# Attention mixer of a two-layer decoder trunk: the norm's scale moved from the qkv weights to the transposed input, the query's norm factor moved into the softmax's scale, the head norms' scales folded into key and cosines

## The chip, the cores and the metric

The kernel runs on one core of a Trainium2 chip. The metric is the device time of one execution in microseconds (us), the median of several runs; lower is better.

## The reference, cut to what matters

Two layers over an input of 256 x 1024 (fp32). Each is: half a gated feed-forward net, a mixer, half a feed-forward net. Layer 0's mixer is a state-space layer, layer 1's is attention with 8 heads of 128. The change touches the attention mixer alone:

```
hn = rms_norm(h, mix_norm[1])                 # h / rms(h) * g, g of 1024
qkv = (hn @ w_qkv).reshape(256, 3, 8, 128)
q = rms_norm(qkv[0], q_gain)                  # over each head's 128, gain of 128
k = rms_norm(qkv[1], k_gain)
q = rope(q, cos, sin) * 128 ** -0.5           # rotates features 0..31, passes 32..127
k = rope(k, cos, sin)
p = softmax(causal(q @ k.T)); o = p @ v;  out = o @ w_out
```

With 256 positions and blocks of 256 there is one block, so the block selection of the reference adds nothing.

## The kernel before, in words

All large products run in three terms. An fp32 operand is split into a high part, rounded to the fast fp32r format, and a low part, the rest; the product is high x high + high x low + low x high. Weights arrive by DMA on the SP queue in units of 1 MB (a tile `raw`, three buffers); `Stream.split` (lines 74 to 98) turns each half unit of 128 x 1024 into `whi` (ScalarE) and `wlo` (VectorE: raw minus whi). A unit that has a gain (the scale of the norm ahead of the product) is scaled on the way, in two pieces of 512 columns, each with its own column of the gain (lines 89 to 94); one without is done in one piece (lines 83 to 87). Splits are issued in program order, by `pump()` at set places and by `get()` where a product needs one that is not there yet.

The residual `h` is transposed by `prep` (line 330): four transposes on TensorE into one PSUM tile, then the high part by ScalarE (342) and the low part by VectorE (343). The factor 1/rms(h) is computed aside (`squares`, `rsq` on GpSimd) and applied when the product leaves PSUM.

`moba` (line 1256) is the attention mixer. It runs twelve chunks in the order k0, q0, k1, q1, v0, v1, each for two row tiles t; a chunk is 128 rows by 512 columns (four heads) and has eight steps k of three products (439 to 441). A chunk with t = 0 meets new weights, one with t = 1 uses the same again. After a chunk ScalarE takes it out of PSUM (`qs`, 1278) and squares each head (1282), and GpSimd makes the head norm's factor `rs` (1283, `rsq` 310 to 314). During the next chunk, ahead of its step 5, `rope` on VectorE multiplies the four heads by factor and gain (1293) and rotates 32 features (1299 to 1304); one chunk later TensorE transposes the result (1314). Scores, their maxima (1324 to 1328), the exponential (1335, 1337), and the product with v are spread over later chunks in slots. Every engine does its work in the order in which the program issues it; nothing is reordered at run time.

Of the kernel before, what the change touches and what calls it, by code (L numbers as in the profile page):

```python
# [10 lines left out]
F32 = mybir.dt.float32  # L11
F32R = mybir.dt.float32r
AF = mybir.ActivationFunctionType
OP = mybir.AluOpType
# [7 lines left out]
EPS = 1e-6  # L22
RAW = 3
HB = 9
NEG = -3.0e38
TWO_PI = 2.0 * math.pi
MAGIC = 12582912.0

# [92 lines left out]
def trunk_kernel(ctx: ExitStack, tc, x, ffn_norm, ffn_w_gate, ffn_w_up, ffn_w_down, mix_norm,  # L121
# [3 lines left out]
    nc = tc.nc  # L125
# [10 lines left out]
    def psM():  # L136
        return pp.tile([128, 512], F32, name="pM", tag="M", bufs=2)

    def psR():
        return pp.tile([128, 512], F32, name="pR", tag="R", bufs=2)  # L140
# [14 lines left out]
    units = []  # L155
    where = {}
    WHOLE = 2
    GAIN = {"f00": None, "f01": 8, "f10": 16, "f11": 24, "s5": 32, "moba": 40}

    def add(key, load, gains=None, whole=False):  # L160

        where[key] = len(units)
        units.append((key, load, gains, whole))
# [27 lines left out]
    def ld_cols(w, r0, c0):  # L191
        def f(t):
            nc.sync.dma_start(t.rearrange("p (k c) -> p k c", c=512),
                              w[r0:r0 + 512, c0:c0 + 512].rearrange("(k p) c -> p k c", p=128))
        return f

    def ffn_units(tag, l, i):
        for j in range(NJ + 1):
            if j < NJ:
                for a in range(2):  # L200
                    add((tag, "g", j, a), ld_gu(l, i, j, a, 2 if j == 0 else 4),
                        GAIN[tag] and GAIN[tag] + 4 * a)
            if j:
                add((tag, "d", j - 1), ld_rows(ffn_w_down[l, i], (j - 1) * 256))

    def s5_units():
        for nh in range(2):
            for a in range(2):
                add(("win", nh, a), ld_cols(s5_w_in[0], a * 512, nh * 512), GAIN["s5"] + 4 * a)
        for key in (('glu', 0), ('glu', 1), ('glu', 2), ('glu', 3), ('so', 0), ('so', 1), ('so', 2), ('so', 3)):  # L210
# [4 lines left out]
    QOFF = {"q": 0, "k": 1024, "v": 2048}  # L215

    def moba_units():
        for kind, hh in QKV:
            for a in range(2):
                add((kind, hh, a), ld_cols(moba_w_qkv[0], a * 512, QOFF[kind] + hh * 512), GAIN["moba"] + 4 * a)  # L220
        for b in range(4):
            add(("mo", b), ld_rows(moba_w_out[0], b * 256))

# [20 lines left out]
    cosT = cst[:, 256:288].rearrange("p (t f) -> p t f", t=2)  # L244
    sinT = cst[:, 288:320].rearrange("p (t f) -> p t f", t=2)
# [45 lines left out]
    gT = cp.tile([128, 48], F32, name="gT")  # L291
# [15 lines left out]
    def rsq(o, v, n):  # L307

        e = sp.tile([128, n], F32, name="rs_e", tag=f"rs_e{n}", bufs=2)
        nc.gpsimd.tensor_tensor(o, v, nhalf[:, 0:n], op=OP.pow)  # L310
        nc.gpsimd.tensor_tensor(e, o, o, op=OP.mult)
        nc.gpsimd.tensor_tensor(e, e, v, op=OP.mult)
        nc.gpsimd.tensor_scalar(e, e, -0.5, 1.5, op0=OP.mult, op1=OP.add)
        nc.gpsimd.tensor_tensor(o, o, e, op=OP.mult)
# [15 lines left out]
    def prep(t, n, ph, sq=True):  # L330

        if (ph, "x") not in X:
            X.clear()
            X[ph, "x"] = True
            X["h"], X["l"] = home(XP[0], ph)
        hh = h[t][:, n * 512:(n + 1) * 512]
        ps = psR()
        pv = ps.rearrange("p (k c) -> p k c", c=128)
        for k in range(4):
            nc.tensor.transpose(pv[:, k, :], hh[:, k * 128:(k + 1) * 128], ident)  # L340
        xh, xl = (X[p][:, n * 4:n * 4 + 4, t * 128:t * 128 + 128] for p in "hl")
        nc.scalar.activation(xh, pv, AF.Copy)
        nc.vector.tensor_tensor(xl, pv, xh.bitcast(F32), op=OP.subtract)
        if sq:
            squares(t, n)

# [909 lines left out]
    def moba(nxt):  # L1256
        V, P = nc.vector, nc.gpsimd
        SCL = 128 ** -0.5
        with tc.tile_pool(name="moba", bufs=1) as wp:
            gq = wp.tile([128, 2, 128], F32, name="gq")  # L1260
            for i, g in enumerate((moba_q_norm, moba_k_norm)):
                nc.sync.dma_start(gq[:, i, :], bass.AP(tensor=g.tensor, offset=g.offset,
                                                       ap=[[0, 128], [1, 128]]))
            vs = [wp.tile([128, D], F32, name=f"vs{t}") for t in range(2)]
            oa = wp.tile([128, 4224], F32R, name="oa")
            oh, ol = (oa[:, OO + 2048 * i:OO + 2048 * i + 2048].rearrange("p (k c) -> p k c", c=256)
                      for i in range(2))
            qkT, QS, QN, SC, PR, PT = {}, {}, {}, {}, {}, {}

            def chunk(kind, hh, t, hooks):  # L1270
                uA, uB = where[kind, hh, 0], where[kind, hh, 1]
                ps = psM()
                product(ps, t, uA, uB, hooks)
                if kind == "v":
                    nc.scalar.activation(halves(vs[t][:, hh * 512:(hh + 1) * 512]), unwoven(ps), AF.Identity, scale=Rr[t])
                    return
                qs = fp.tile([128, 512], F32, name="qs", tag="gr", bufs=2)
                nc.scalar.activation(halves(qs), unwoven(ps), AF.Identity, scale=Rr[t])
                ss = wp.tile([128, 4], F32, name="qss", bufs=2)
                sq = wp.tile([128, 128], F32, name="qsq", bufs=1)  # L1280
                for i in range(4):
                    nc.scalar.activation(sq, qs[:, i * 128:(i + 1) * 128], AF.Square, accum_out=ss[:, i:i + 1])
                P.tensor_scalar(ss, ss, 1.0 / 128, EPS, op0=OP.mult, op1=OP.add)
                rs = wp.tile([128, 4], F32, name="qrs", bufs=2)
                rsq(rs, ss, 4)
                QS[kind, hh, t] = (qs, rs)

            def rope(kind, hh, t):
                qs, rs = QS.pop((kind, hh, t))
                qn = wp.tile([128, 4, 128], F32, name="qn", bufs=2)  # L1290
                g = gq[:, 0 if kind == "q" else 1, :]
                for i in range(4):
                    V.scalar_tensor_tensor(qn[:, i, :], qs[:, i * 128:(i + 1) * 128], rs[:, i:i + 1], g,
                                           op0=OP.mult, op1=OP.mult)
                x1, x2 = qn[:, :, 0:16], qn[:, :, 16:32]
                cb = cosT[:, t, None, :].to_broadcast([128, 4, 16])
                sb = sinT[:, t, None, :].to_broadcast([128, 4, 16])
                m = [wp.tile([128, 4, 16], F32, name=f"rp{i}", bufs=1) for i in range(4)]
                V.tensor_tensor(m[0], x1, cb, op=OP.mult)
                V.tensor_tensor(m[1], x2, sb, op=OP.mult)  # L1300
                V.tensor_tensor(m[2], x2, cb, op=OP.mult)
                V.tensor_tensor(m[3], x1, sb, op=OP.mult)
                V.tensor_tensor(x1, m[0], m[1], op=OP.subtract)
                V.tensor_tensor(x2, m[2], m[3], op=OP.add)
                QN[kind, hh, t] = qn
# [11 lines left out]
            def scores(hd):  # L1317
                hh, i = divmod(hd, 4)
                q, k = qkT["q", hh], qkT["k", hh]
                ps = psA(i)  # L1320
                mm(ps[:, 0:128], q[:, i, 0:128], k[:, i, 0:128], start=True, stop=True)
                mm(ps[:, 128:384], q[:, i, 128:256], k[:, i, 0:256], start=True, stop=True)
                dv = ps.rearrange("p (a c) -> p a c", c=256)[:, :, 0:128]
                V.tensor_tensor(dv, dv, cmask[:, None, :].to_broadcast([128, 2, 128]), op=OP.add)
                mx = wp.tile([128, 2], F32, name="mx", bufs=3)
                V.reduce_max(mx[:, 0:1], ps[:, 0:128], axis=AX.X)
                V.reduce_max(mx[:, 1:2], ps[:, 128:384], axis=AX.X)
                V.tensor_scalar(mx, mx, -SCL, None, op0=OP.mult)
                SC[hd] = (ps, mx)

            def expo(hd):
                ps, mx = SC.pop(hd)
                pr = wp.tile([128, 384], F32, name="pr", bufs=4)
                sm = wp.tile([128, 2], F32, name="sm", bufs=4)
                nc.scalar.activation(pr[:, 0:128], ps[:, 0:128], AF.Exp, bias=mx[:, 0:1], scale=SCL,
                                     accum_out=sm[:, 0:1])
                nc.scalar.activation(pr[:, 128:384], ps[:, 128:384], AF.Exp, bias=mx[:, 1:2], scale=SCL,
                                     accum_out=sm[:, 1:2])
                PR[hd] = (pr, sm)

# [32 lines left out]
            for hd in range(8):  # L1373
                g = 24 + 4 * hd if hd < 4 else 30 + 2 * hd
# [104 lines left out]
    ps = psR()  # L1479
# [31 lines left out]
def host_consts():  # L1511
# [3 lines left out]
    pos = 4 * (r % 32) + r // 32  # L1515
    c[:, 128:256] = np.where(pos[None, :] <= pos[:, None], 0.0, NEG).astype(np.float32)
    inv = (500000.0 ** (-np.arange(0, 32, 2, dtype=np.float64) / 32)).astype(np.float32)
# [34 lines left out]
```

## Time and profile before

| | |
|---|---|
| median of 3 runs | 925.89 us (921.27 to 927.68) |
| the profiled execution | 926.08 us, of which the span is 924.3 |
| TensorE (PE) | 914.9 us, 99% of the span |
| VectorE (DVE) | 719.0 us, 78% |
| ScalarE (ACT) | 587.0 us, 64% |
| GpSimd (POOL) | 222.7 us, 24% |
| TensorE clock granted, mean | 0.997 |

The span runs from the first instruction to the last. Busy shares are means over stages that differ; the attention mixer's projections lie at 642 to 720 us, its output product follows up to about 747.

### The profile page before, as it was taken

What the parts mean: (1) busy time and instruction counts of PE and PEld (TensorE: products, weight loads), DVE (VectorE), ACT (ScalarE), POOL (GpSimd) and SP (SyncE); (2) the same over time, 40 slices, a digit from 0 to 9 for tenths busy, and PEclk for the clock granted to TensorE, in tenths of its full rate; (3) what the DMA queues carried; (4) which work ended last, traced back from release to release, by engine and by line L of the source; (5) the groups of instructions that cost most, each with busy time, mean ns of one, the idle gap of its engine ahead of it and who ended that gap; (6) DMA issues with size and microseconds to landing.
All of it is one profiled execution on the core that took longest, in us unless ns stands there. A gap on an engine that the chain in (4) does not pass through costs nothing.

```text
span 924.3 us, 15612 instructions
## 1 busy us (share of the span) xinstructions
PE 914.9 (99%) x5772; PEld 817.9 (88%) x5772; DVE 719.0 (78%) x1235; ACT 587.0 (64%) x1122; POOL 222.7 (24%) x389
## 2 busy tenths in 40 slices
PE   9999999999999999999999999999999999999998
PEld 7888878898999999999999999999888899999997
DVE  6899877868877888777678887776789668887773
ACT  7665756654376666666466666665898666676651
POOL 6992879924812000000020000001441020000000
PEclk9999999999999999999999999999999999999999
DMA  9999999988746766565637666563554647656531
GB/s 286 277 294 334 331 265 273 301 282 322 287 158 197 235 224 231 186 227 183 183 126 238 228 194 216 186 224 97 182 164 156 195 135 252 234 187 227 182 137 46
DMA packets 145388, 200.75 MB, mean 217 GB/s; under 512 B 20168, under 2 KB 117408, under 8 KB 145056
## 3 DMA queue, kind: packets, MB, share of 16 engines
q1 hardware_dynamic: 137744, 188.24, 62.6%
q0 software_dynamic: 6848, 10.72, 4.3%
q10 hardware_dynamic: 720, 0.80, 0.3%
q8 instruction: 45, 0.74, 0.3%
q14 instruction: 31, 0.25, 0.1%
HBM read 183.82 MB, written 15.76 MB: 216 GB/s over the span
## 4 chain that ended last, share of the span: by engine, by line
PE 89%; DMA 3%; POOL 2%; issue 2%; DVE 2%; ACT 1%; SPq 0%; ACTq 0%; DVEq 0%; POOLq 0%
PE pR L589 11%; PE pM L589 11%; PE pA L425 10%; PE pA L426 10%; PE pA L427 10%; PE pR L591 5%; PE pM L591 5%; PE pM L425 4%; PE pM L426 4%; PE pM L427 4%; PE pM L595 2%; PE pM L596 2%; PE pM L594 2%; DMA dA<-t 2%; PE pR L1118 1%
## 5 line engine op out<-in xcount | busy, mean ns | idle before, releaser
L93 DVE SCALAR_TENSOR_TENSOR wlo<-raw,gT,whi 128x512 fp32r<-128x512 f32 x328 | 228.0, 747 | 41.9 <-ACT whi L92 41.7
L87 DVE TENSOR_TENSOR wlo<-raw,whi 128x1024 fp32r<-128x1024 f32 (+1 forms) x155 | 188.0, 1233 | 41.4 <-ACT whi L86 37.0
L92 ACT ACTIVATE whi<-raw,gT 128x512 fp32r<-128x512 f32 x328 | 212.9, 710 | 3.5 <-PE pA L427 2.1
L86 ACT ACTIVATE whi<-raw 128x1024 fp32r<-128x1024 f32 (+1 forms) x155 | 158.5, 1045 | 38.3 <-DMA raw<-in_ffn_w_up_dram 25.5
L589 PE MATMUL pR<-xa,whi 128*128 128x512 f32 x456 | 174.2, 382 | 0.0
L589 PE MATMUL pM<-xa,whi 128*128 128x512 f32 x456 | 174.0, 382 | 0.0
L425 PE MATMUL pA<-whi,ah 128*128 128x512 f32 x352 | 134.9, 383 | 0.0
L426 PE MATMUL pA<-wlo,ah 128*128 128x512 f32 x352 | 133.7, 380 | 0.0
L427 PE MATMUL pA<-whi,al 128*128 128x512 f32 x352 | 133.6, 379 | 0.0
L591 PE MATMUL pR<-xa,wlo 128*128 128x256 f32 x456 | 124.3, 273 | 0.0
L591 PE MATMUL pM<-xa,wlo 128*128 128x256 f32 x456 | 124.3, 273 | 0.0
L355 POOL TENSOR_TENSOR ms<-ss 128x1 f32<-128x1 f32 x10 | 3.5, 348 | 435.4 <-ACT sq L352 435.4
L589 PEld LDWEIGHTS pR<-xa,whi 128*128 128x128 f32 x456 | 86.2, 189 | 12.2
L589 PEld LDWEIGHTS pM<-xa,whi 128*128 128x128 f32 x456 | 86.2, 189 | 11.9
L591 PEld LDWEIGHTS pM<-xa,wlo 128*128 128x128 f32 x456 | 87.4, 192 | 1.4
L591 PEld LDWEIGHTS pR<-xa,wlo 128*128 128x128 f32 x456 | 87.6, 192 | 0.0
L618 ACT ACTIVATE sg<-gr 128x256 f32<-128x256 f32 x66 | 27.5, 417 | 87.2 <-DVE gr L611 61.6
L425 PE MATMUL pM<-whi,xa 128*128 128x512 f32 (+1 forms) x208 | 79.9, 384 | 0.0
L426 PE MATMUL pM<-wlo,xa 128*128 128x512 f32 (+1 forms) x208 | 76.2, 366 | 0.1
L427 PE MATMUL pM<-whi,xa 128*128 128x512 f32 (+1 forms) x208 | 76.1, 366 | 0.0
L427 PEld LDWEIGHTS pA<-whi,al 128*128 128x128 f32 x352 | 66.7, 189 | 9.5
L425 PEld LDWEIGHTS pA<-whi,ah 128*128 128x128 f32 x352 | 66.8, 190 | 9.3
(290 smaller groups left out, 1745.1 us busy)
## 6 DMA issues: line engine op xcount, KB each, us to landing
raw<-in_ffn_w_down_dram SPq DMA_DIRECT2D x44, 1024.0 KB, 5.5
raw<-in_ffn_w_gate_dram SPq DMA_DIRECT2D x80, 512.0 KB, 4.0
raw<-in_ffn_w_up_dram SPq DMA_DIRECT2D x80, 512.0 KB, 5.1
raw<-in_moba_w_qkv_dram SPq DMA_DIRECT2D x12, 1024.0 KB, 5.2
TB<-dB SPq DMA_DIRECT2D x8, 768.0 KB, 7.0
dA<-blank SPq DMA_DIRECT2D x8, 512.0 KB, 10.2
dB<-tt POOLq DMA_DIRECT2D x16, 256.0 KB, 7.5
raw<-in_s_w_in_dram SPq DMA_DIRECT2D x4, 1024.0 KB, 9.7
```

Source lines behind the costliest of these rows:

```text
L86: nc.scalar.activation(hi[:, c], r[:, c], AF.Copy)
L87: nc.vector.tensor_tensor(lo[:, c], r[:, c], hi[:, c].bitcast(F32), op=OP.subtract)
L92: nc.scalar.activation(hi[:, c], r[:, c], AF.Identity, scale=g)
L93: nc.vector.scalar_tensor_tensor(lo[:, c], r[:, c], g, hi[:, c].bitcast(F32), op0=OP.mult, op1=OP.subtract)
L425: mm(o, xh, wh, start=start, stop=False)
L426: mm(o, xh, wl, start=False, stop=False)
L427: mm(o, xl, wh, start=False, stop=stop)
L589: mm(ps[i], a, XB[:, :, k, :].rearrange("p i (t c) -> p i c t", t=2), start=k == 0, stop=False, skip_group_check=True)
L591: mm(ps[i][:, 0:256], b, xh, start=False, stop=k == 7, skip_group_check=True)
L594: mm(o, a, xh, start=k == 0 and i == 0, stop=False, skip_group_check=True)
L595: mm(o, a, xl, start=False, stop=False, skip_group_check=True)
L618: nc.scalar.activation(sg, gr[:, 0, :], AF.Silu)
```

## The change

The gain of the attention mixer's norm leaves the weight split (its units have none now, and are split in one piece) and goes to `prep`: for this phase each of the four transposed blocks is scaled by its own column of the gain, in four instructions on ScalarE and four on VectorE in place of one each. The query is no longer multiplied by its norm factor and gain: `rope` rotates `qs` in place. The factor, times 128 ** -0.5, goes to a small tile `scl` (one more GpSimd step), which is the scale of the exponential and of the maxima. For the 96 features that are not rotated the query's gain is multiplied into the key's (`gk`); for the 32 rotated ones each gain goes into its own cosines and sines (`cs`). These two tables are made by ten GpSimd instructions at the start of `moba`. The mask's constant is smaller in size, as it is scaled now.

```
-    GAIN = {"f00": None, "f01": 8, "f10": 16, "f11": 24, "s5": 32, "moba": 40}
+    GAIN = {"f00": None, "f01": 8, "f10": 16, "f11": 24, "s5": 32, "moba": None}
...
-                add((kind, hh, a), ld_cols(moba_w_qkv[0], a * 512, QOFF[kind] + hh * 512), GAIN["moba"] + 4 * a)
+                add((kind, hh, a), ld_cols(moba_w_qkv[0], a * 512, QOFF[kind] + hh * 512))
...
-        nc.scalar.activation(xh, pv, AF.Copy)
-        nc.vector.tensor_tensor(xl, pv, xh.bitcast(F32), op=OP.subtract)
+        if ph == "moba":
+            for k in range(4):
+                g = gT[:, 40 + 4 * n + k:41 + 4 * n + k]
+                nc.scalar.activation(xh[:, k, :], pv[:, k, :], AF.Identity, scale=g)
+                nc.vector.scalar_tensor_tensor(xl[:, k, :], pv[:, k, :], g, xh[:, k, :].bitcast(F32),
+                                               op0=OP.mult, op1=OP.subtract)
+        else:
+            nc.scalar.activation(xh, pv, AF.Copy)
+            nc.vector.tensor_tensor(xl, pv, xh.bitcast(F32), op=OP.subtract)
...
+            gk = wp.tile([128, 128], F32, name="gk")
+            P.memset(gk[:, 0:32], 1.0)
+            P.tensor_tensor(gk[:, 32:128], gq[:, 0, 32:128], gq[:, 1, 32:128], op=OP.mult)
+            cs = wp.tile([128, 2, 4, 2, 16], F32, name="cs")
+            for i in range(2):
+                for m, (tr, c) in enumerate(((cosT, 0), (sinT, 16), (cosT, 16), (sinT, 0))):
+                    P.tensor_tensor(cs[:, i, m], tr, gq[:, i, None, c:c + 16].to_broadcast([128, 2, 16]), op=OP.mult)
...
+                if kind == "q":
+                    if t == 0:
+                        SQ[hh] = wp.tile([128, 4, 2], F32, name="scl", bufs=2)
+                    P.tensor_scalar(SQ[hh][:, :, t], rs, SCL, None, op0=OP.mult)
...
-                qn = wp.tile([128, 4, 128], F32, name="qn", bufs=2)
-                g = gq[:, 0 if kind == "q" else 1, :]
-                for i in range(4):
-                    V.scalar_tensor_tensor(qn[:, i, :], qs[:, i * 128:(i + 1) * 128], rs[:, i:i + 1], g,
-                                           op0=OP.mult, op1=OP.mult)
+                qn = qs.rearrange("p (i c) -> p i c", c=128)
+                if kind == "k":
+                    for i in range(4):
+                        V.scalar_tensor_tensor(qn[:, i, :], qn[:, i, :], rs[:, i:i + 1], gk, op0=OP.mult, op1=OP.mult)
...
-                V.tensor_scalar(mx, mx, -SCL, None, op0=OP.mult)
+                V.scalar_tensor_tensor(mx, mx, -1.0, SQ[hh][:, i, :], op0=OP.mult, op1=OP.mult)
...
-                nc.scalar.activation(pr[:, 0:128], ps[:, 0:128], AF.Exp, bias=mx[:, 0:1], scale=SCL,
+                nc.scalar.activation(pr[:, 0:128], ps[:, 0:128], AF.Exp, bias=mx[:, 0:1], scale=sc[:, 0:1],
```

## Rows read from the trace of the kernel before

**Rows 1.** The page, busy time by engine over the whole span.
```profile
PE 914.9 (99%) x5772; PEld 817.9 (88%) x5772; DVE 719.0 (78%) x1235; ACT 587.0 (64%) x1122; POOL 222.7 (24%) x389
```

**Rows 2.** Table by stage: length, busy PE, PEld, DVE, ACT, POOL, clock, DMA, GB/s.
```profile
642.00:700.00 58.00, 57.17 (x287) 48.77 (x286) 46.92 (x136) 52.73 (x139) 26.42 (x60) 1.00 0.49 159
700.00:740.00 40.00, 40.00 (x207) 35.19 (x206) 31.93 (x70) 26.49 (x57) 0.00 (x0) 1.00 0.55 181
```

**Rows 3.** Waits of the weight loads, 640 to 750 us: total, times, longest.
```profile
PEld pM L441 <- DVE wlo L93: 2.4, 4, 0.7
```

**Rows 4.** TensorE in order of time: start, duration, instruction, at the four waits.
```profile
655.70 0.38 PE L439 MATMUL pM<-whi,xa 128*128 128x512 f32 x1
655.91 0.38 PE L440 MATMUL pM<-whi,xa 128*128 128x512 f32 x1
656.54 0.48 PE L441 MATMUL pM<-wlo,xa 128*128 128x512 f32 x1 [0.24 <-DVE wlo L93]
...
667.66 0.38 PE L440 MATMUL pM<-whi,xa 128*128 128x512 f32 x1
668.10 0.48 PE L441 MATMUL pM<-wlo,xa 128*128 128x512 f32 x1
...
681.62 0.38 PE L440 MATMUL pM<-whi,xa 128*128 128x512 f32 x1
682.19 0.48 PE L441 MATMUL pM<-wlo,xa 128*128 128x512 f32 x1 [0.19 <-DVE wlo L93]
...
695.38 0.38 PE L440 MATMUL pM<-whi,xa 128*128 128x512 f32 x1
696.08 0.48 PE L441 MATMUL pM<-wlo,xa 128*128 128x512 f32 x1 [0.33 <-DVE wlo L93]
```

**Rows 5.** Groups by line, 632 to 737 us: busy, mean ns, idle before.
```profile
L93 DVE SCALAR_TENSOR_TENSOR wlo<-raw,gT,whi 128x512 fp32r<-128x512 f32 x47 | 32.7, 746 | 4.1 <-ACT whi L92 4.1
L87 DVE TENSOR_TENSOR wlo<-raw,whi 128x1024 fp32r<-128x1024 f32 x8 | 9.6, 1222 | 5.3 <-ACT whi L86 5.3
...
L92 ACT ACTIVATE whi<-raw,gT 128x512 fp32r<-128x512 f32 x48 | 31.6, 715 | 0.0
L1282 ACT ACTIVATE qsq<-qs 128x128 f32<-128x128 f32 x32 | 9.9, 310 | 1.4
L86 ACT ACTIVATE whi<-raw 128x1024 fp32r<-128x1024 f32 x8 | 8.2, 1047 | 0.0
```

**Rows 6.** VectorE in order of time, 651 to 696 us; xN: merged neighbours.
```profile
651.26 1.42 DVE L93 SCALAR_TENSOR_TENSOR wlo<-raw,gT,whi 128x512 fp32r<-128x512 f32 x2 [2.81 <-ACT whi L92]
653.62 1.14 DVE L1293 SCALAR_TENSOR_TENSOR qn<-qs,qrs,gq 128x128 f32<-128x128 f32 x4 [0.94 <-POOL qrs L314]
...
665.18 1.14 DVE L1293 SCALAR_TENSOR_TENSOR qn<-qs,qrs,gq 128x128 f32<-128x128 f32 x4 [0.93 <-POOL qrs L314]
...
689.99 1.14 DVE L1293 SCALAR_TENSOR_TENSOR qn<-qs,qrs,gq 128x128 f32<-128x128 f32 x4
...
695.28 1.41 DVE L93 SCALAR_TENSOR_TENSOR wlo<-raw,gT,whi 128x512 fp32r<-128x512 f32 x2
```

**Rows 7.** GpSimd in order of time, around the mixer's first chunk.
```profile
646.94 0.19 POOL L314 TENSOR_TENSOR rr<-rr,rs_e 128x1 f32<-128x1 f32 x1
650.70 0.20 POOL L1283 TENSOR_SCALAR qss<-qss 128x4 f32<-128x4 f32 x1 [3.57 <-ACT qsq L1282]
...
652.08 0.65 POOL L311 TENSOR_TENSOR rs_e<-qrs 128x4 f32<-128x4 f32 x1
```

**Rows 8.** GpSimd, line 741: ns min/median/max, first and last start, forms.
```profile
L741 POOL TENSOR_TENSOR e<-sc x4: 238/685/1217, 36.1 to 41.9; 128x32 f32<-128x32 f32 x4
...
L741 POOL TENSOR_TENSOR e<-e,e x2: 251/284/318, 44.0 to 45.4; 128x32 f32<-128x32 f32 x2
```

**Rows 9.** ScalarE's and TensorE's instructions for the fourth half, in time.
```profile
644.37 1.32 ACT L92 ACTIVATE whi<-raw,gT 128x512 fp32r<-128x512 f32 x2
...
647.06 0.38 PE L441 MATMUL pM<-wlo,xa 128*128 128x512 f32 x1
```

More of the change, by code (lines that the diff above doesn't have):

```diff
@@ L24 @@
 HB = 9
-NEG = -3.0e38
+NEG = -1.0e30
 TWO_PI = 2.0 * math.pi
@@ L1267, in moba @@
                       for i in range(2))
-            qkT, QS, QN, SC, PR, PT = {}, {}, {}, {}, {}, {}
+            qkT, QS, QN, SC, PR, PT, SQ = {}, {}, {}, {}, {}, {}, {}
             def chunk(kind, hh, t, hooks):
@@ L1289, in rope @@
                 qs, rs = QS.pop((kind, hh, t))
-                qn = wp.tile([128, 4, 128], F32, name="qn", bufs=2)
-                g = gq[:, 0 if kind == "q" else 1, :]
-                for i in range(4):
-                    V.scalar_tensor_tensor(qn[:, i, :], qs[:, i * 128:(i + 1) * 128], rs[:, i:i + 1], g,
-                                           op0=OP.mult, op1=OP.mult)
+                qn = qs.rearrange("p (i c) -> p i c", c=128)
+                if kind == "k":
+                    for i in range(4):
+                        V.scalar_tensor_tensor(qn[:, i, :], qn[:, i, :], rs[:, i:i + 1], gk, op0=OP.mult, op1=OP.mult)
                 x1, x2 = qn[:, :, 0:16], qn[:, :, 16:32]
-                cb = cosT[:, t, None, :].to_broadcast([128, 4, 16])
-                sb = sinT[:, t, None, :].to_broadcast([128, 4, 16])
+                c1, s2, c2, s1 = (cs[:, "qk".index(kind), k, t, None, :].to_broadcast([128, 4, 16]) for k in range(4))
                 m = [wp.tile([128, 4, 16], F32, name=f"rp{i}", bufs=1) for i in range(4)]
[L1299 to L1302, printed above, removed]
+                V.tensor_tensor(m[0], x1, c1, op=OP.mult)
+                V.tensor_tensor(m[1], x2, s2, op=OP.mult)
+                V.tensor_tensor(m[2], x2, c2, op=OP.mult)
+                V.tensor_tensor(m[3], x1, s1, op=OP.mult)
                 V.tensor_tensor(x1, m[0], m[1], op=OP.subtract)
@@ L1332, in expo @@
                 ps, mx = SC.pop(hd)
+                sc = SQ[hd // 4][:, hd % 4, :]
                 pr = wp.tile([128, 384], F32, name="pr", bufs=4)
                 sm = wp.tile([128, 2], F32, name="sm", bufs=4)
-                nc.scalar.activation(pr[:, 0:128], ps[:, 0:128], AF.Exp, bias=mx[:, 0:1], scale=SCL,
+                nc.scalar.activation(pr[:, 0:128], ps[:, 0:128], AF.Exp, bias=mx[:, 0:1], scale=sc[:, 0:1],
                                      accum_out=sm[:, 0:1])
-                nc.scalar.activation(pr[:, 128:384], ps[:, 128:384], AF.Exp, bias=mx[:, 1:2], scale=SCL,
+                nc.scalar.activation(pr[:, 128:384], ps[:, 128:384], AF.Exp, bias=mx[:, 1:2], scale=sc[:, 1:2],
                                      accum_out=sm[:, 1:2])
```

## The prediction

> **What bounds the kernel now.** I read the page's first part, then a table of the stretch that the change touches, then the waits of TensorE there, then the instructions around each wait. The first part says that TensorE is busy for 99% of the span [rows 1]. An average can hide a stage with another limit, so the second look is at the attention mixer's projections and scores, 642 to 700 us: TensorE 57.17 of 58.00 us, ScalarE 52.73, VectorE 46.92, GpSimd 26.42, clock 1.00 [rows 2]. TensorE bounds this stage too; the other engines are close behind it and are late now and then. How often? The list of waits has one entry that counts: the third product of a step (the one that reads wlo) waited for VectorE's split four times, 2.4 us at the weight loads [rows 3]. The four places are seen as a late start after the second product: 0.63, 0.44, 0.57 and 0.70 us where 0.215 is usual, so 0.41 + 0.22 + 0.35 + 0.48 = 1.5 us lost [rows 4]. They lie in the chunks 2, 4, 6 and 8 of the mixer's twelve, those that meet new weights. Everything the change takes off ScalarE, VectorE and GpSimd can come back only through these four waits: at most 1.5 us of 926 by the starts, 2.4 by the weight loads.
>
> **The sum starts from the profiled run**, 926.08 us (924.3 of span and 1.8 around it), which is 0.2 above the median of 925.89; the three runs shown lie between 921.27 and 927.68.
>
> **Part by part.** *Weight split without gain.* Twenty-four halves of the qkv weights each cost two 128x512 pieces now. A pair takes 1.41 us on VectorE [rows 6] and 1.32 on ScalarE [rows 9]; a whole 128x1024 takes 1.222 and 1.047 [rows 5]. That is about 0.2 and 0.3 us per half, some 4.6 and 7 us in all, none of it on TensorE's path by itself. The other side: the first products of a half wait for its first 512 columns only, ready 0.746 after a start, and will now wait for all 1024, 1.222: **+0.48 us of latency** wherever TensorE waits for a split that has just begun.
>
> *Scale on the transposed input.* Four preparations change from one 128x512 instruction on each engine to four of 128x128. The nearest rows are 0.310 for a 128x128 against 0.715 for a 128x512 on ScalarE, and 1.14 for four against 0.746 on VectorE [rows 5, 6]: +0.5 and +0.4 us each. TensorE's inputs for these are wanted microseconds later, so that is covered; but the split of chunk 0's fourth half is queued behind. Its whi began at 644.37 and TensorE wanted its wlo at 647.06 [rows 9]. With 0.5 of delay: 644.87 + 1.05 + 1.22 = 647.14, so **+0.1 us**; between 0 (the delay is smaller) and 0.5 (VectorE's share too).
>
> *Query without its four multiplies.* 1.14 us go from each of four query ropes, and with them VectorE's wait for GpSimd's factor. In chunk 4 the late split stood behind the query rope that began at 665.18, after 0.93 us of waiting for GpSimd [rows 6]; VectorE is free about 1 us earlier and saves 1.14, more than the 0.48 of latency. **-0.2 us.** In chunk 8 the split at 695.28 stood behind such a rope begun at 689.99; 1.14 and two cheaper splits (0.4) go, 0.48 comes. **-0.5 us.**
>
> *Key ropes keep their multiplies.* In chunk 6 the late split comes after a key rope and the scores' maxima: 0.2 cheaper ahead of it, 0.48 longer itself, **+0.2 us** (0 to 0.3). The scaled cosines replace plain ones in equal shapes: nothing.
>
> *Ten instructions on GpSimd* (a fill, a product of 128x96, eight of 128x32), queued behind the second norm factor, which ends at 646.94 + 0.19 = 647.1 [rows 7], and ahead of the first key factor's chain, which began at 650.70 and released the rope at 653.62. This is the unknown that matters: behind it stand the key factor, then the rope on VectorE, then the split that chunk 2 waits for. The cost of one is bracketed by the same shape earlier in the trace: 0.25 to 0.32 us in quiet, 1.2 where it is slow [rows 8]. With 0.08 between: ten quiet ones take 3.6 us; starting at 647.4 (the squares before them are a little later) they end at 651.0. I add one slow one, 0.9, since a single split runs on VectorE in that stretch, and it then stands idle for 2.81 us before 651.26 [rows 6]: 651.9, so 1.2 us late. Chunk 2's wait grows by 1.2 + 0.48: **+1.7 us**, between +0.5 (no lateness) and +11 (all ten slow). I stay near the low end because of that idle time. The ten also wait for the loads of the two norm vectors, which are issued at the same place as now. The first rope reads them, and what it waited for last was GpSimd's factor [rows 6]: they cost nothing then; should they land after 647 they would push the ten back by as much, which the upper end has room for.
>
> That a split slows GpSimd is seen in a row: its product at 652.08 took 0.65 and ended within 0.1 us of the pair of splits begun at 651.26; another short product, at 646.94, took 0.19 [rows 6, 7]. The Trainium skill has a rule for it (SBUF — State Buffer, section Who interferes with whom): a VectorE instruction with two inputs in SBUF and a GpSimd instruction that reads SBUF exclude each other, and the later one waits until the first is done. The trace agrees in that one row. By the rule each whole split that meets the ten stops them once; by a rule that let them run side by side the term would be +0.8.
>
> *Exponential and maximum.* Sixteen exponentials get their scale from a tile in place of a constant, eight small VectorE steps change kind, two small GpSimd steps per query half come in. Bounds: nothing, or 0.1 to 0.2 us each. From 700 to 740 us TensorE is busy 40.00 of 40.00 [rows 2] while ScalarE's pieces fit between; if that cover went, 1 to 2 us. I take nothing. The tiles of the stage move by some 1.5 KB; the trace shows no instruction whose time hangs on its place, so nothing, either way.
>
> Sum: 0.1 - 0.2 - 0.5 + 0.2 + 1.7 = +1.3: 926.1 + 1.3 = 927.4 beside the profiled run, **927.2** beside the median.
>
> **Rivals.** *Relief wins* (0.2): the key ropes too find GpSimd in time, no split is waited for, all four waits go. -1.5 us, 924.4 (2.4 gone: 923.5). For it: all three engines lose work. Against it: chunk 2's wait came with two chains in a row, and neither gets shorter. *GpSimd holds the first key* (0.17), the slower side: the ten are slow because VectorE's splits run beside them. At a mean of 0.8 they end near 656.2, 5.5 late, +5.6 in all: 931.5. At 1.2 or above they end 9 late, and the kernel is over 1% slower, 935 to 938; a mean of 1.2 is the point from which it decides. For it: in an earlier stage the median of four was 0.685 and the slowest 1.217 [rows 8]. Against it: here VectorE stands idle for most of the time in question. I give 0.13 to the first and 0.04 to the second. *The forecast* has 0.61. *The query still waits* (0.02): its rope writes over the tile that ScalarE's squares read, so if those ended as late as GpSimd's factor, nothing would be gained in chunks 4 and 8: 927.9.
>
> **How the numbers follow.** About 1%, 9 us, is what a measurement can tell from no change. Faster by that would take six times the waiting that TensorE does here: 0.02, out of the first rival's 0.2, for what I have not seen. Slower by it: 0.04, the end of the GpSimd rival. Within it: 0.94. The range takes the forecast, most of both rivals, and a median that can lie where the shown runs lie: 922.5 to 932.
>
> **What would show it.** Right: TensorE's wait in chunk 2 longer by 1 to 2 us and its third product released by the split; none in chunks 4 and 8; ten GpSimd rows between 647 and 652; TensorE's busy time the same. Wrong: no wait in chunk 2 (the latency term fails), a first key factor begun after 654 (the GpSimd term is mis-sized), or a product pitch other than 0.215 us (place matters after all).

## The result, and the profile after

The changed kernel takes 932.56 us (931.47 to 935.99, six runs) where the kernel before, timed beside it, takes 925.51: 7.05 us more, 0.8% by the two medians. The ratio on record, which is not the quotient of the medians, is 1.0103 with a 95% interval of [1.0082, 1.0123]. The profiled execution took 933.07, its span is 931.4. The forecast, 927.2, had the sign and a fifth of the size (+1.3), and its range ended at 932.0.

The page's first part of the changed kernel answers to [rows 1], in the same columns.

```profile
PE 916.2 (98%) x5772; PEld 818.9 (88%) x5772; DVE 714.1 (77%) x1207; ACT 584.1 (63%) x1110; POOL 223.1 (24%) x403
```

VectorE and ScalarE lost 4.9 and 2.9 us of work, as the change says. TensorE has the same 5772 instructions and only 1.3 us more of busy time, in a span 7.1 longer: it waits. Where? The table by stage answers to [rows 2]; its last two rows look closer (length, busy PE, PEld, DVE, ACT, POOL, clock, DMA, GB/s).

```profile
642.00:700.00 58.00, 51.81 (x245) 43.49 (x244) 37.10 (x98) 44.83 (x116) 29.61 (x69) 0.97 0.43 139
700.00:740.00 40.00, 39.84 (x210) 34.84 (x210) 29.64 (x70) 29.34 (x64) 2.84 (x7) 1.00 0.47 156
660.00:665.00 5.00, 2.79 (x9) 2.35 (x10) 4.31 (x12) 1.90 (x3) 3.50 (x6) 0.72 0.58 190
665.00:670.00 5.00, 5.00 (x24) 4.33 (x23) 2.21 (x8) 3.48 (x11) 0.57 (x2) 0.94 0.53 201
```

From 642 to 700 us TensorE issues 245 products where it issued 287, while every other engine but GpSimd is busy for less: nobody is the bound, they wait for each other. A measure that does not depend on where a stage lies is the time from the first transpose of the mixer's input to the first one behind the mixer, both at line 340. I call it the **stage**. In the kernel before, and then in the changed one:

```profile
637.75 0.60 PE L340 MATMUL pR<-cst,h 128*128 128x128 f32 x4
...
740.70 0.60 PE L340 MATMUL pR<-cst,h 128*128 128x128 f32 x4
```

```profile
636.68 0.60 PE L340 MATMUL pR<-cst,h 128*128 128x128 f32 x4
...
747.74 0.60 PE L340 MATMUL pR<-cst,h 128*128 128x128 f32 x4
```

The stage is 111.06 us long, against 102.95 before. That is +8.11; the stretch ahead of it, which the change does not touch, came out 1.07 shorter in this execution.

The waits of the weight loads, 630 to 760 us, answer to [rows 3]:

```profile
PEld pM L448 <- DVE wlo L87: 5.9, 6, 3.1
PEld pR L340 <- DVE h L386: 2.3, 2, 1.7
PEld pM L446 <- ACT whi L86: 1.7, 1, 1.7
```

The first is the old wait, larger. The other two did not exist before: TensorE's transposes wait for `h`, which VectorE writes (386), and chunk 0's products wait for a high part. TensorE in order of time shows each place (start, duration, instruction):

```profile
640.58 0.38 PE L434 MATMUL pA<-whi,al 128*128 128x512 f32 x1
641.14 0.66 PE L340 MATMUL pR<-cst,h 128*128 128x128 f32 x4 [0.19 <-DVE h L386]
...
642.72 0.38 PE L448 MATMUL pM<-wlo,xa 128*128 128x512 f32 x1
644.41 0.66 PE L340 MATMUL pR<-cst,h 128*128 128x128 f32 x4 [1.32 <-DVE h L386]
...
647.28 0.38 PE L448 MATMUL pM<-wlo,xa 128*128 128x512 f32 x1
648.95 0.48 PE L446 MATMUL pM<-whi,xa 128*128 128x512 f32 x1 [1.29 <-ACT whi L86]
649.27 0.38 PE L447 MATMUL pM<-whi,xa 128*128 128x512 f32 x1
650.21 0.48 PE L448 MATMUL pM<-wlo,xa 128*128 128x512 f32 x1 [0.56 <-DVE wlo L87]
...
659.16 0.38 PE L447 MATMUL pM<-whi,xa 128*128 128x512 f32 x1
662.21 0.80 PE L448 MATMUL pM<-wlo,xa 128*128 128x512 f32 x1 [2.67 <-DVE wlo L87]
...
664.50 0.63 PE L448 MATMUL pM<-wlo,xa 128*128 128x512 f32 x1
664.93 0.63 PE L446 MATMUL pM<-whi,xa 128*128 128x512 f32 x1
```

By the starts, with the usual pitch (from one start to the next) of 0.215 taken off: 0.34, 1.47, 1.45 and 0.72 at the entry of the stage, 4.0 in all, where nothing was lost before; 2.83 in chunk 2 against 0.41, so 2.4 more. Behind that last wait the pitch is 0.43 (664.50 to 664.93), twice the usual, in the slices where the granted clock is 0.72 and 0.94: TensorE had stood idle and ran at 1.2 GHz before it ran at 2.4 again. That is another 1.6 us (measured in the last experiment). 4.0 + 2.4 + 1.6 = 8.0 of the 8.11. The later chunks balance: chunk 4's wait is gone but for 0.19, chunks 6 and 8 still lose 0.49 and 0.33, 1.0 in all against 1.05 before [rows 4].

Why are VectorE and ScalarE late at the entry, with less to do? VectorE in order of time, the first preparation (the number in brackets is the idle time before, and who ended it):

```profile
637.71 0.35 DVE L346 SCALAR_TENSOR_TENSOR xa<-pR,gT,xa 128x128 fp32r<-128x128 f32 x1 [0.65 <-ACT xa L345]
638.50 0.35 DVE L346 SCALAR_TENSOR_TENSOR xa<-pR,gT,xa 128x128 fp32r<-128x128 f32 x1 [0.44 <-ACT xa L345]
...
643.62 0.74 DVE L386 SCALAR_TENSOR_TENSOR h<-pA,half,h 128x512 f32<-128x512 f32 x1
```

And ScalarE, the same preparation, then what stood behind the fourth:

```profile
638.10 0.37 ACT L345 ACTIVATE xa<-pR,gT 128x128 fp32r<-128x128 f32 x1 [0.42 <-DVE xa L346]
638.89 0.37 ACT L345 ACTIVATE xa<-pR,gT 128x128 fp32r<-128x128 f32 x1 [0.42 <-DVE xa L346]
...
652.29 1.05 ACT L86 ACTIVATE whi<-raw 128x1024 fp32r<-128x1024 f32 x1
653.23 0.68 ACT L1292 ACTIVATE qs<-pM,rr 128x512 f32<-128x512 f32 x1
```

VectorE's wait for ScalarE is data: the low part of a block needs its high part. ScalarE's wait for VectorE is not: block k+1 of ScalarE reads nothing that VectorE's block k writes. They read the same PSUM tile, though, and take turns at it: one block of each in 0.785 us (638.10 to 638.89), of which 0.42 to 0.44 is idle on either engine. A preparation lasts some 3.2 us; before it was one piece of 0.60 and then one of 0.69.

### The profile page after: what moved, and what is told of

Same layout as the page of the kernel before. It is cut to its first block, busy times and chain, and to the rows that moved or that the text cites. A ratio compares the mean times of both kernels' runs of the same rounds, so it can differ in the third digit from the quotient of the medians.

```text
span 931.4 us, 15583 instructions
## 1 busy us (share of the span) xinstructions
PE 916.2 (98%) x5772; PEld 818.9 (88%) x5772; DVE 714.1 (77%) x1207; ACT 584.1 (63%) x1110; POOL 223.1 (24%) x403
## 4 chain that ended last, share of the span: by engine, by line
PE 82%; DMA 6%; POOL 4%; ACT 3%; DVE 3%; issue 1%; SPq 0%; ACTq 0%; DVEq 0%
PE pR L596 11%; PE pM L596 11%; PE pA L432 9%; PE pA L434 9%; PE pA L433 9%; PE pM L598 5%; PE pR L598 5%; DMA dA<-t 4%; PE pM L432 2%; PE pM L434 2%; PE pM L433 2%; DMA raw<-in_ffn_w_up_dram 2%; PE pM L602 2%; PE pM L603 2%; PE pM L601 2%; PE pM L448 1%
## 5 line engine op out<-in xcount | busy, mean ns | idle before, releaser
L87 DVE TENSOR_TENSOR wlo<-raw,whi 128x1024 fp32r<-128x1024 f32 (+1 forms) x179 | 217.3, 1232 | 54.4 <-ACT whi L86 50.2
L93 DVE SCALAR_TENSOR_TENSOR wlo<-raw,gT,whi 128x512 fp32r<-128x512 f32 x280 | 194.6, 747 | 37.5 <-ACT whi L92 37.3
L86 ACT ACTIVATE whi<-raw 128x1024 fp32r<-128x1024 f32 (+1 forms) x179 | 183.1, 1045 | 40.4 <-DMA raw<-in_ffn_w_up_dram 21.1
L92 ACT ACTIVATE whi<-raw,gT 128x512 fp32r<-128x512 f32 x280 | 181.3, 709 | 3.5 <-PE pA L434 2.1
```

What stands on the lines that cost most here:

```text
L86: nc.scalar.activation(hi[:, c], r[:, c], AF.Copy)
L87: nc.vector.tensor_tensor(lo[:, c], r[:, c], hi[:, c].bitcast(F32), op=OP.subtract)
L92: nc.scalar.activation(hi[:, c], r[:, c], AF.Identity, scale=g)
L93: nc.vector.scalar_tensor_tensor(lo[:, c], r[:, c], g, hi[:, c].bitcast(F32), op0=OP.mult, op1=OP.subtract)
```

## The experiments

**Theory A**: the turns in the preparation make VectorE and ScalarE late, and all else (the entry's waits, the first key, chunk 2, the clock) follows. **The rival, B**, seeks the loss in the other half of the change, the first key's chain with GpSimd's ten new instructions. Each kernel was timed beside the kernel before; the ratios are to that. The expectations in microseconds go by the 925.51 of the first comparison; the kernel before took 923.13 beside experiments 1 to 4, 923.41 beside 5 to 8 and 923.49 beside 9 and 10. A stage is read from one execution of each kernel.

**1. The input's part alone.** The gain moves to the preparation; query, key and softmax stay as before.

```
 kernel before
-GAIN = {... "moba": 40}
+GAIN = {... "moba": None}     # and prep in four scaled blocks
```

> Theory A (turn-taking): in the changed kernel ScalarE's block k+1 of a preparation waits for VectorE's block k, since both read one PSUM bank, and each of the four preparations takes 3.2 us in place of 1.2; nearly all of the loss comes from there. The kernel before with this part alone, query and key as they were, is then slower by 5 to 9 us, like the whole change. Theory B (the tables made on GpSimd and the new rope hold the first key): this part alone costs 0 to 2 us.

930.97, ratio 1.008 [1.0064, 1.0095], stage 110.94. Nearly the whole loss is here, without GpSimd's ten. A holds, B falls. (This part holds the turns and the whole splits together; experiments 7 and 9 take them apart.)

That the two stages agree within 0.12 us is in part luck. The waits at the entry are the same to 0.01 us, but here the clock had fallen behind them, long before chunk 2:

```profile
650.00:655.00 5.00, 5.00 (x18) 4.12 (x18) 1.94 (x4) 4.79 (x13) 1.12 (x2) 0.74 0.53 196
...
660.25 0.48 PE L448 MATMUL pM<-wlo,xa 128*128 128x512 f32 x1 [0.96 <-DVE wlo L87]
```

With TensorE slowed down ahead of it, chunk 2 lost 1.12 by the starts in place of 2.83. The chunks 4 to 8 of this kernel, which keeps the query's multiplies, lost 2.4 in place of 1.0.

**2. The query's and key's part alone.** The other half.

```
 changed kernel
-GAIN = {... "moba": None}
+GAIN = {... "moba": 40}       # and prep in one piece per engine
```

> The changed kernel with the gain back in the weight split and the old preparation. Theory A: the loss is gone, 924 to 927 us, no wait in chunks 4 and 8, the wait in chunk 2 as before (0.4 us) as GpSimd's tables end before the first key factor is asked for. Theory B: still 929 us or more, with a wait of over 1 us in chunk 2.

922.32, ratio 0.998 [0.9966, 0.9994], stage 101.70 (-1.25): faster than both kernels, than the one before by 0.2%. Its waits of the weight loads, against the four and 2.4 of [rows 3]:

```profile
PEld pM L441 <- DVE wlo L93: 1.3, 3, 0.6
```

**3. Two banks.** The four blocks of a preparation go to two PSUM tiles in turn, nothing else.

```
 changed kernel
-ps = psR(); pv = four blocks of ps
+two = [psR(), psR() if (t, n) == (1, 1) else psM()]
+pv = [two[k % 2][:, k * 128:(k + 1) * 128] for k in range(4)]
```

> The changed kernel with the four transposed blocks of a preparation put in two PSUM banks in turn (no instruction added). Theory A: ScalarE and VectorE no longer take turns, a preparation takes about 2 us or less, the waits at the transposes and in chunk 0 go, chunk 2 waits under 1.5 us: 925 to 928 us. If the turn-taking comes from the tile that both write to (high and low part lie in one), nothing changes: 932 us.

923.78, 1.0011 [0.9996, 1.0027], stage 104.24. ScalarE in order of time:

```profile
634.50 0.37 ACT L350 ACTIVATE xa<-pR,gT 128x128 fp32r<-128x128 f32 x1 [2.94 <-PE pR L345]
634.77 0.36 ACT L350 ACTIVATE xa<-pM,gT 128x128 fp32r<-128x128 f32 x1
635.29 0.37 ACT L350 ACTIVATE xa<-pR,gT 128x128 fp32r<-128x128 f32 x1 [0.16 <-DVE xa L351]
635.55 0.36 ACT L350 ACTIVATE xa<-pM,gT 128x128 fp32r<-128x128 f32 x1
```

The second block, in the other tile, starts at once (0.27 after the first); the third, back in the first tile, waits for VectorE. The tile `xa`, which all blocks write, is the same for all four, so it is not what they wait for. It is the PSUM tile.

**4. Four, then four.** One tile, but all of ScalarE's blocks are issued ahead of VectorE's.

```
 changed kernel
 for k in range(4): nc.scalar.activation(block k)
+for k in range(4):
     nc.vector.scalar_tensor_tensor(block k)
```

> The changed kernel with ScalarE's four blocks issued ahead of VectorE's four, in one bank as before. Theory A: one handover in place of seven, a preparation takes 2.2 to 2.5 us in place of 3.2, and a third to a half of the loss comes back: 928 to 930 us. Theory B: no change, 932 us.

924.32, 1.0014 [1.0002, 1.0026], stage 103.59: better than the 928 to 930 expected (1.0014 times 925.51 is 926.8). VectorE:

```profile
634.85 1.13 DVE L347 SCALAR_TENSOR_TENSOR xa<-pR,gT,xa 128x128 fp32r<-128x128 f32 x4 [1.43 <-ACT xa L345]
```

I had counted the two fours as a delay of VectorE. They take 1.14 and 1.13 us with one hand-over, and while VectorE has its four, ScalarE goes on with other work; no transpose waited for `h` in this run.

**5 and 6. The rope one slot later.** Are the late splits of [rows 4] late only because a rope stands ahead of them? Once in the kernel before, once in that of experiment 2.

```
-at(4 * (i + 1) + 2, rope, *prods[i])
+at(4 * (i + 1) + 3, rope, *prods[i])
```

> The kernel before with one number changed: the rotation of a query or key is issued ahead of step 7 of the next chunk, behind the weight split pumped after step 5, and not ahead of step 5. Measured from the first transpose of the mixer's input to the first transpose behind the mixer, the stage takes 102.95 us in the kernel before. Theory: a split waits because VectorE has the rope queued ahead of it. Then the waits in chunks 2 and 4 go (0.41 and 0.22 us and what follows), those in 6 and 8, whose split is pumped after the rope in any case, stay: 102.2 to 102.5. If the splits are late by themselves: 102.9 or more.

> The query part alone (stage 101.70 us) with the rope behind that split too. Theory: the wait left in chunk 2 goes, the stage takes 101.0 to 101.5 us, and the kernel is faster than before by 1.5 to 2 us. If GpSimd's factor holds the key rope so long that the next split is late as well: 101.7 or more.

926.53, 1.0027 [1.001, 1.0044], stage 105.88; and 924.03, 1.0004 [0.9987, 1.002], stage 103.93. Both expectations fell: the stages lie on the side of the other outcome that each had named, but not for its reason. Waits of the weight loads in the first of them:

```profile
PEld pR L1314 <- issue: 3.4, 2, 2.0
PEld pR L1314 <- DVE qn L1304: 1.2, 2, 0.9
PEld pM L441 <- DVE wlo L93: 0.7, 1, 0.7
```

The splits are in time now, with one exception, and the transposes of the rope's result (1314) wait in their place. The slots of before were a balance between the two.

**7. The splits in halves again,** without gain, on top of experiment 4: the latency term by itself.

```
-n = 512 if self.ns == 0 else 1024
+n = 512 if self.ns == 0 or self.units[u][0][0] in ("k", "q", "v") else 1024
```

> The changed kernel with the four blocks grouped by engine (stage 103.59 us), and the qkv weights split in two pieces of 512 columns again, without gain. The prediction's latency term: the wait in chunk 2 falls from 1.0 to 0.5 us, and the stage to 102.6 to 103.1 us, though ScalarE and VectorE get 7 and 4.6 us more work. If piece size does not matter: 103.6 or more.

922.52, 0.9988 [0.9968, 1.0007], stage 101.55, so -2.04 against experiment 4. TensorE in chunk 2:

```profile
655.03 0.38 PE L448 MATMUL pM<-whi,xa 128*128 128x512 f32 x1
655.89 0.48 PE L449 MATMUL pM<-wlo,xa 128*128 128x512 f32 x1 [0.48 <-DVE wlo L87]
```

Chunk 2's wait went from 1.0 to 0.65 (0.86 less 0.215), and those in the chunks 0, 4, 6 and 8 (0.2, 0.2, 0.5 and 0.33) are gone: 1.6 of the 2.04 by the starts.

**8. The products of the cosine table three times over,** on top of experiment 4: the GpSimd term by itself.

```
-for i in range(2):
+for i in (0, 1, 0, 1, 0, 1):
```

> The changed kernel grouped by engine, with GpSimd's eight products for the cosine table made three times over (sixteen more, the same values). The prediction's GpSimd term: with no slack left in front of the first key factor each us of them is a us of wait in chunk 2; sixteen at 0.25 to 0.34 make it 4 to 5.5 us longer, and the stage 107.5 to 110 us. If the tables are off the path: 103.6 us.

A single run: 933.36 (923.41 before), stage 110.6, just above the range expected, +7.0 against experiment 4. GpSimd and TensorE in experiment 4:

```profile
643.74 2.70 POOL L1278 TENSOR_TENSOR cs<-cst,gq 128x32 f32<-128x32 f32 x8
646.52 0.20 POOL L1298 TENSOR_SCALAR qss<-qss 128x4 f32<-128x4 f32 x1
...
651.51 0.38 PE L448 MATMUL pM<-whi,xa 128*128 128x512 f32 x1
652.74 0.48 PE L449 MATMUL pM<-wlo,xa 128*128 128x512 f32 x1 [0.85 <-DVE wlo L87]
```

and in experiment 8:

```profile
648.09 7.05 POOL L1278 TENSOR_TENSOR cs<-cst,gq 128x32 f32<-128x32 f32 x24
...
655.87 0.38 PE L448 MATMUL pM<-whi,xa 128*128 128x512 f32 x1
661.10 0.80 PE L449 MATMUL pM<-wlo,xa 128*128 128x512 f32 x1 [4.85 <-DVE wlo L87]
```

The tables take 4.35 longer and chunk 2's pitch grows from 1.23 to 5.23, 4.0; the rest is the slower clock behind a wait that long (0.54 and 0.78 granted from 660 to 665 and from 665 to 670 us). In experiment 4 the first key factor began right at the tables' end, so there the chain had no slack, and the GpSimd term is real: what is added to the tables comes back nearly microsecond for microsecond.

**9. Four blocks in turn, unscaled, in the kernel before.** Neither gain nor whole splits nor GpSimd's ten: the turns alone.

```
 kernel before
-nc.scalar.activation(xh, pv, AF.Copy); nc.vector.tensor_tensor(xl, pv, xh, subtract)
+for k in range(4): the same two for block k
```

> The kernel before with nothing changed but the shape of the mixer's four preparations: four blocks of 128 columns per engine, issued in turn as in the changed kernel, without a gain; the gain stays in the weight split. Theory A (turn-taking in one bank is the loss): a preparation takes 3.2 us, TensorE waits at the transposes and in chunk 0, and the stage grows from 102.95 to between 107 and 110 us. If the gain moved to this place, or the whole split, is what costs: under 104 us.

928.07, 1.0043 [1.0024, 1.0062], stage 108.57 (+5.6). ScalarE and, below, TensorE in chunk 2:

```profile
636.67 0.28 ACT L344 ACTIVATE xa<-pR 128x128 fp32r<-128x128 f32 x1 [0.36 <-DVE xa L345]
637.30 0.28 ACT L344 ACTIVATE xa<-pR 128x128 fp32r<-128x128 f32 x1 [0.36 <-DVE xa L345]
...
654.88 0.38 PE L445 MATMUL pM<-whi,xa 128*128 128x512 f32 x1
657.75 0.48 PE L446 MATMUL pM<-wlo,xa 128*128 128x512 f32 x1 [2.50 <-DVE wlo L93]
```

The turns take 0.63 us each here and make most of the loss by themselves: 5.6 of 8.11 by the stage, 4.6 of 7.05 us by the medians. At the entry this run loses 1.7 by the starts, though, and not 4.0; the rest comes with the longer turns of scaled blocks and with the whole splits, which no run takes apart there.

**10. Chunk 2's wait filled.** Twelve products of 128x512 that nobody reads, ahead of the product that waits: the clock's share.

```
 changed kernel
+if t == 0 and k == 4 and uA == where["q", 0, 0]:
+    fl = psR()
+    for i in range(12): mm(fl, xh, woven(wh[:, c]), start=i == 0, stop=i == 11)
 mm(o, xh, woven(wl[:, c]), ...)
```

> The changed kernel with twelve more 128x512 products (2.6 us of TensorE's time, into a PSUM tile that nothing reads) put into the 2.8 us wait of chunk 2, so that TensorE hardly stands idle there. In the changed kernel the products behind that wait ran at 0.43 us in place of 0.215 for about 3 us, at a granted clock of 0.72 for 5 us. Theory: the low clock follows the idle time and costs 1.5 to 2 us by itself; then the stage falls from 111.1 to 109 to 109.6 us though TensorE has more work. If the clock falls in any case (the earlier waits suffice): 111 us or more.

930.39, 1.007 [1.005, 1.009], stage 109.42: 1.64 less than the changed kernel's, with twelve products more. The product that had waited starts 25.54 us into the stage (25.53 in the changed kernel), so all of the difference lies behind it. The slice that had a clock of 0.72, in the table by stretch:

```profile
660.00:665.00 5.00, 4.92 (x25) 4.01 (x25) 4.28 (x13) 2.60 (x7) 3.56 (x6) 1.00 0.58 205
```

and the products, in TensorE's order of time:

```profile
660.24 2.75 PE L451 MATMUL pR<-whi,xa 128*128 128x512 f32 x12
```

Not tried: to let both engines read one PSUM tile at once, by taking away the wait itself; experiment 3 takes away its cause instead.

## Why the prediction was wrong

**The step that failed is "Scale on the transposed input"**, +0.1 us. It priced four preparations as the sum of their pieces (+0.5 and +0.4 us) and held them covered, since TensorE's inputs "are wanted microseconds later". The pieces are hardly dearer than I said: 0.37 us each for 0.310 on ScalarE, and VectorE's four take 1.13 with nothing between them (experiment 4) for 1.14. What I left out is the hand-overs: the program issues ScalarE, VectorE, ScalarE, VectorE on one PSUM tile, and each waits for the other, eight pieces in a row. A preparation got 2 us longer, not 0.5. And the cover was not asked for everything that it hides: it held for `xa`, but VectorE's queue holds the next half of `h` behind the turns (643.62), which TensorE transposes at once, and ScalarE's queue holds the high part of a weight and the first chunk's eviction. Of these the prediction had named the weight alone, chunk 0's fourth half, with 0.5 of delay: it began 11.18 us into the stage (647.86 less 636.68) and not 6.62 (644.37 [rows 9] less 637.75), 4.6 later. In all the entry lost 4.0. The first key factor began 19.06 into the stage (655.74 less 636.68), not 12.95 (650.70 [rows 7] less 637.75): 6.1 later, the 4.0 and some 2 of ScalarE's queue, and these 2 came back in chunk 2.

The Trainium skill has a rule that I had not weighed (PSUM — Partial Sum Buffer, section PSUM bank collisions raise a hardware error): two different engines may not access the same bank, in the same partitions, at the same time, readers included, and the order is kept by software, which makes one instruction depend on the other. The trace agrees as far as the order goes: ACT 345 waits for DVE 346 without sharing data, and stops doing so with the blocks in two tiles (experiment 3). What a collision would do, no run here shows.

**Clock.** No term for it; in the profiled execution it cost 1.64 (experiment 10) behind a wait of 2.83. The waits of before, 0.48 at most by the starts, had not lowered it [rows 2, 4], nor did one of 1.50 in experiment 3. But its place is not settled by one wait: behind the same waits at the entry it stayed at 1.00 up to chunk 2 in the changed kernel and fell in experiment 1 (0.74 from 650 to 655 us).

**Weight split without gain** (+0.48 of latency in chunk 2). The sign holds; in chunk 2 it is 0.35. But it is paid in other chunks too, 2.0 in all on top of experiment 4. I had set it against the relief in the chunks 4 and 8, and in chunk 8 it nearly ate that: -0.15 (0.48 to 0.33) instead of -0.5. Chunk 6 came out at +0.14 (0.35 to 0.49) for the +0.2 said, chunk 4 at -0.03 (0.22 to 0.19) for -0.2.

**Query without its multiplies.** Right: with the splits as before, the query's part alone takes 1.25 us off the stage (experiment 2).

**GpSimd's ten.** In the changed kernel the term is zero, not 1.2: its chain came so late for the other reason that GpSimd stood idle for 2.62 us ahead of the first key factor.

```profile
651.39 1.73 POOL L1277 TENSOR_TENSOR cs<-cst,gq 128x32 f32<-128x32 f32 x8
655.74 0.20 POOL L1297 TENSOR_SCALAR qss<-qss 128x4 f32<-128x4 f32 x1 [2.62 <-ACT qsq L1296]
```

The rival that came nearest in time, "GpSimd holds the first key" with 931.5, is thus not what happened. As a mechanism it is real once the turns are gone (experiment 8), but the sum had it too large: in experiment 4 one of the eight products took 1.23 us, just the one slow one that the sum allows, and the factor waited for the tables some 0.2, not 1.2 (ScalarE's last square ended at 646.20 and the factor began at 646.52; before, 650.61 and 650.70). The upper end of +11 is a slip as well: ten at 1.2 with 0.08 between end at 660.2, 9.5 late, so some +10.

Of the prediction's signs of success, chunk 2's wait was released by the split, as it said, but grew by 2.4 and not by 1 to 2, and for another reason; the chunks 4 and 8 still waited, and the ten ran from 650.96 to 653.12, not between 647 and 652. A first key factor begun after 654 was the sign against it, and that is what came, from ScalarE and not from GpSimd.

**Exponentials, maxima, the tiles' places.** Right: the exponentials took longer (below), from chunk 8's wait to the end of the stage it takes 44.46 us (44.62 before) with TensorE busy throughout, and the pitch is 0.215 where the clock is full.

## What to carry to other kernels

When one instruction is cut into several that two engines issue in turn on the same PSUM tile, price the hand-overs, not the pieces: here 0.42 us of idle time per turn on either engine, 3.2 us in place of 1.3. Issue all of one engine's pieces first, or alternate between two tiles. And before calling a delay covered, list everything queued behind it on that engine, not only its own result: the part that paid here was another tile's, one place down the queue.

## What the runs showed of the hardware that I had not expected

An exponential whose scale comes from a tile is dearer by 0.09 us: 0.453 and 0.556 us for 128 and 256 columns, against 0.366 and 0.466 before with a constant. It is hidden here: 16 x 0.09 = 1.4 us on an engine with room.

The same eight GpSimd products took 1.73 us in the changed kernel, where no split ran on VectorE beside them, and 2.70 in experiment 4, where one ran from 643.45 to 644.85: there one of the eight took 1.23, while the median is 0.25 in both runs.
